# A transformer block on one core: operand roles of the dilation-16 value products, and where the merge factors are applied

## The chip, the cores and the metric

The kernel runs on one core of a Trainium2 chip. Time is device time in microseconds of one launch. A run of this kernel repeats closely: three runs before gave 2552.69, 2554.15 and 2554.9 us, and the median, 2554.15, is the time to be compared. The engines are named as the profile names them: TensorE (PE for the matrix products, PEld for the loads of their weights, the stationary operand), VectorE (DVE), ScalarE (ACT), GpSimd (POOL) and SyncE (SP); the last two start the transfers.

## The reference

One decoder block on 2048 positions of width 1024, all in float32. Its first half normalises the input and projects it once. The columns are shared by two groups of heads: four heads of gated linear attention, and eight softmax heads of width 64 that look at their keys at three dilations. Both results pass one output projection. The second half is a gated feed-forward layer of width 2816 with a causal convolution of width 3.

The change touches the softmax heads alone. For each of the dilations 1, 4 and 16 a query attends to 128 keys back at most, in steps of the dilation. The three results are merged by their softmax denominators:

```python
    s = jnp.where(valid, s + alibi, -jnp.inf)
    m = jnp.max(s, axis=-1, keepdims=True)
    p = jnp.exp(s - m)
    den = jnp.sum(p, axis=-1, keepdims=True)
    o = jnp.einsum('bdhnqk,bdhnke->bdhnqe', p, vw.astype(jnp.float32)) / den
    lse = (m + jnp.log(den))[..., 0]
...
    weights = jax.nn.softmax(jnp.stack(lses, axis=0), axis=0)
    return jnp.einsum('gbsh,gbshe->bshe', weights, jnp.stack(outs, axis=0))
```

So for each query, head and dilation there is one factor, exp(m - M) / (sum over dilations of den * exp(m - M)), by which the unnormalised product of p with the values is multiplied before the three are added. Since it belongs to the query, it may multiply p ahead of the product, or the product behind it.

## The kernel before

**Blocks and streams.** The 2048 positions go in four blocks of 512 (`c` from 0 to 3, `NCH`). For each block there is a projection (`proj`), the mixing (`mix`: two steps of linear attention, `gla`, and then `attn` four times, for the four pairs of softmax heads, `hp`), the output projection (`outproj`) and the feed-forward layer (`ffn`). The wide products of `proj`, `outproj`, `ffn` and `down` all go through `mm3` (lines 318 to 320): each float32 operand is split into a high and a low part, and three products of 128 x 128 by 512 columns take the place of one. They fill most of TensorE's time.

**What sets the order.** `mix` and the wide work are generators. `beside` (line 115) walks through the two in turn: a step of `mix` up to its next `yield`, then a step or more of wide work. This gives the written order. The order that each engine really gets is worked out by a planner that runs over the whole program as it is compiled (line 39): it works with a model of the engines' times, and may put instructions that are free to go ahead of written ones that still wait. Each engine then carries out its own instructions in the order it was given. TensorE's small products of `attn` stand in one queue with the wide ones.

**One pair of heads in `attn`.** Tiles have 128 partitions. `s16[hh]` holds the scores of head `hh` (0 or 1) at dilation 16, with 128 queries on the partitions (32 j + l) and four groups `r4` of `nk` = 32 (c + 1) keys in the free dimension; query position 16 l + 4 j + r4. `s4` and `sn` hold the scores of dilations 4 and 1 for both heads, in 4 x 384 columns: 4 x 192 of each head, or 128 where there are no keys before.

1. Scores are made on TensorE (lines 939 and 888), biased with their maxima taken on VectorE (`TTR`, line 903), and turned to exponentials on ScalarE (`soft`, line 907).
2. The maxima and denominators of dilation 1 and 4 are brought to the query order of dilation 16 (lines 978 to 987, with small products at 981 and 983), and the factors `f` for all three dilations are worked out (lines 988 to 997) on VectorE and ScalarE. Line 997 finishes `f`.
3. In the same step `s16` is transposed on TensorE, four transposes of 128 queries by `nk` keys for each head (`turn` at line 1002, which the profile shows as line 916 with tile `s`), and copied back into `s16` as keys by queries (line 1002, by way of `copy`, lines 195 and 197). This is not dependent on `f`.
4. After a `yield`, the factors of dilations 1 and 4 are brought back to these dilations' own query orders (lines 1005 to 1007, 1017 and 1018). `scale` (line 1009) multiplies `s4` and `sn` by them in place: for each head and each of the four groups one instruction with a scalar per partition (line 1013), 8 for each call, 16 for each pair of heads.
5. `turns` transposes `s4` and `sn` (line 916 with tile `sx`), with a `yield` after each.
6. The value products. Those of dilation 16 (line 1037) have the 32 queries of one (r4, j) as the stationary operand and the 64 values as the moving one. The output is 32 queries (partitions 32 j and up) by 64 values. With two heads, four r4 and four j there are 32 of them; j is the innermost loop. Those of dilations 4 and 1 (`add`, line 1043) have the values as the stationary operand, so that their outputs `O` and `O1` have values on the partitions, the two heads on halves of them.
7. `weigh` (line 1021, its multiplication is line 1025) multiplies the dilation-16 output by its factor, from PSUM into a buffer of the ring `pt`. After a `yield` four transposes (line 1064) bring it to values by queries, ScalarE copies it to the tile `stage` in position order (line 1066), and VectorE adds `O1` and `O` to that (lines 1067 and 1069). The result is stored for `outproj`.

PSUM tiles of `attn` and `gla` come from a pool of four (`psa`), the wide products' from another of four (`psg`).

Of the kernel before, what the change touches and what calls it, by code (L numbers as in the profile page):

```python
# [11 lines left out]
F32 = mybir.dt.float32  # L12
# [3 lines left out]
ALU = mybir.AluOpType  # L16
# [4 lines left out]
P = 128  # L21
T = 512
# [126 lines left out]
class K:  # L149
# [687 lines left out]
    def attn(self, c, hp, ready):  # L837
        nc, D = self.nc, self.D
        nk = 32 * (c + 1)
# [29 lines left out]
        s16 = [self.at.tile([P, T], F32, name="s16", bufs=2) for _ in range(2)]  # L869

        H = [slice(0, 64), slice(64, P)]
# [40 lines left out]
        def turn(n, b0, part, to):  # L912

            ps = self.pa()
            for i in range(b0, 4):
                nc.tensor.transpose(ps[:n, i * P:(i + 1) * P], part(i), self.C("id"))  # L916
            self.copy(to, ps[:n, b0 * P:].rearrange("p (r n) -> p r n", n=P))

        def turns(t, first):

            for k in range(3):
                n = slice(k * P, (k + 1) * P)
                b0 = sum(map(first, range(4))) if k == 1 else 0
                if b0 < 4:
                    turn(P, b0, lambda i: t[:, i, n], t[:, b0:, n])
# [9 lines left out]
        for r4 in range(4):  # L935
            for j in range(4):
                for hh in range(2):
                    r = 4 * j + r4
# [4 lines left out]
        v16 = self.at.tile([P, 16, P], F32, name="v16", tag="kt", bufs=2)  # L943
# [13 lines left out]
        ends = lambda *a: (lambda lo, n: (lo, lo + n))(*span(*a))  # L957
# [32 lines left out]
        f = self.at.tile([P, 2, 3, 4], F32, name="f", bufs=2)  # L990
# [8 lines left out]
        xm = self.at.tile(x4, F32, name="xm", bufs=2)[:, 0:2]  # L999
        nc.vector.tensor_tensor(xm, f[:, :, 2][:, :, None, :].to_broadcast(x2), self.C("s4")[:, None, :, None].to_broadcast(x2), op=ALU.mult)  # L1000
        for hh in range(2):
            turn(nk, 0, lambda i: s16[hh][:, i * nk:(i + 1) * nk], s16[hh][:nk].rearrange("p (r n) -> p r n", n=P))
        yield
        ps = self.pa()
# [2 lines left out]
        nc.vector.tensor_copy(f[:, :, 1], ps[:, 32:40].rearrange("p (a r) -> p a r", r=4))  # L1007

        def scale(t, g, first):
            for hh in range(2):  # L1010
                for i in range(4):
                    lo, hi = ends(i, hh, first, g)
                    nc.vector.tensor_scalar(t[:, i, lo:hi], t[:, i, lo:hi], f[:, hh, g, i:i + 1], None, op0=ALU.mult)

        scale(s4, 1, z4)
        xm = self.at.tile(x4, F32, name="xm", bufs=2)[:, 0:2]
        nc.vector.tensor_tensor(xm, ps[:, 0:32].rearrange("p (a b r) -> p a b r", b=4, r=4), self.C("s1")[:, None, None, :].to_broadcast(x2), op=ALU.mult)
        nc.vector.tensor_reduce(f[:, :, 2], xm, AX.X, ALU.add)
        scale(sn, 2, z1)

        def weigh(out, g):

            t = self.at.tile([P, T], F32, name="pt", tag="pt", bufs=5)
            v = lambda t: t.rearrange("p (r h n) -> p r h n", r=4, h=2)
            nc.vector.tensor_tensor(v(t), v(out), f[:, :, g].rearrange("p h r -> p r h")[:, :, :, None].to_broadcast([P, 4, 2, 64]), op=ALU.mult)
            return t

        cols = lambda r4, hh: slice((2 * r4 + hh) * 64, (2 * r4 + hh + 1) * 64)
        turns(s4, z4)
        yield  # L1030
        turns(sn, z1)
        yield
        O16 = self.pa()
        for hh in range(2):
            for r4 in range(4):
                for j in range(4):
                    nc.tensor.matmul(O16[32 * j:32 * j + 32, cols(r4, hh)], s16[hh][:nk, r4 * P + 32 * j:r4 * P + 32 * j + 32], v16[:nk, 4 * j + r4, H[hh]], start=True, stop=True, skip_group_check=True)  # L1037
        O, O1 = self.pa(), self.pa()
        first = [True] * 4

        def add(o, hh, out, lhsT, rhs):
            k = 2 * (o is o1) + hh
            nc.tensor.matmul(out, lhsT, rhs, start=first[k], stop=False, skip_group_check=True)  # L1043
            first[k] = False
# [8 lines left out]
        for i in range(4):  # L1053
            for z in range(2):
                for o, t, vf, only, g in ((o4, s4, f4, z4, 1), (o1, sn, f1, z1, 2)):
                    for hh in range(2):
                        R = H[place(hh, g)]
                        if not only(i):
                            add(o, hh, o(hh, i)[:, z], vf[R, i, z], t[R, i, P + 64 * z:P + 64 * z + 64])
        acc = weigh(O16, 0)  # L1060
        yield
        O16 = self.pa()
        for r4 in range(4):
            nc.tensor.transpose(O16[:, r4 * P:(r4 + 1) * P], acc[:, r4 * P:(r4 + 1) * P], self.C("id"))
        st = self.at.tile([P, T], F32, name="stage", bufs=2)
        nc.scalar.copy(st.rearrange("p (l j r) -> p r j l", j=4, r=4), O16.rearrange("p (r j l) -> p r j l", r=4, j=4))
        nc.vector.tensor_tensor(st, O1, st, op=ALU.add)
# [301 lines left out]
```

## Time and profile before

| | |
|---|---|
| median of the three runs | 2554.15 us |
| the profiled execution's own time | 2554.95 us |
| its span, first to last instruction | 2553.2 us |
| TensorE products busy | 2529.3 us (99% of the span), 19458 instructions |
| TensorE weight loads busy | 2086.9 us (82%) |
| VectorE busy | 1891.1 us (74%), 4104 instructions |
| ScalarE busy | 1279.0 us (50%) |
| GpSimd busy | 446.5 us (17%) |
| granted TensorE clock | 1.000 |

The profile is of one execution. A row of the groups reads: line, engine, operation, written tile <- read tiles, for TensorE the size of the stationary operand (rows * columns), output partitions x columns, and the count; then the busy time in us and the mean duration of one in ns; then the idle time of the engine ahead of these instructions with what ended it. Products overlap in the array: one record's duration runs from its start to its modelled end, and the next may start long before that, so the busy time of a group is not its count times the mean. A row of the timeline is start and length in us, engine, line, operation, tiles and a count for neighbours put together (with the form of the first). A row of the waits is the engine, tile and line that waited, what it waited for, and then the total in us, the number of times and the longest. A row of a stretch gives its length and, for each engine in the order PE, PEld, DVE, ACT, POOL, busy time and count, then the TensorE clock, the share of the DMA engines and GB/s.

### The profile page before, as it was taken

To read this page: it belongs to the slowest core of one execution; us is meant where nothing else is said; L and a number is where in the kernel's file an instruction comes from. 1 tells how busy PE (TensorE), PEld (TensorE's weight loads), DVE (VectorE), ACT (ScalarE), POOL (GpSimd) and SP (SyncE) were. 2 spreads that over 40 slices of the span, in tenths; PEclk is the share of its full clock that TensorE was granted. 3 is DMA by queue.
4 is the path that set the end of the run, shared out by engine and by line. 5 is a ranking of instruction groups with operands and counts; after the bars stand their busy time and mean duration, and the time that the engine had idled before them with its cause. 6 is when DMAs were issued, how large, how long until landed. Compare 5 with 4: busy or idle time off the path is not lost.

```text
span 2553.2 us, 49701 instructions
## 1 busy us (share of the span) xinstructions
PE 2529.3 (99%) x19458; PEld 2086.9 (82%) x19458; DVE 1891.1 (74%) x4104; ACT 1279.0 (50%) x2633; POOL 446.5 (17%) x814
## 2 busy tenths in 40 slices
PE   7999999999999999999999999999999999999999
PEld 4888888888788888888888888888888888888887
DVE  7678877767788677787977777779777776766665
ACT  5566665666554544454545544445444443433332
POOL 2343332322210000122100000310000003100001
PEclk9999999999999999999999999999999999999999
DMA  8776676665632344455434445643444436432332
GB/s 329 251 259 199 203 250 198 215 202 183 219 120 93 120 142 134 131 190 174 130 120 129 136 145 152 208 150 101 125 147 140 146 104 202 149 98 93 99 99 83
DMA packets 189582, 406.30 MB, mean 159 GB/s; under 512 B 48498, under 2 KB 89380, under 8 KB 188068
## 3 DMA queue, kind: packets, MB, share of 16 engines
q0 software_dynamic: 88096, 308.59, 36.9%
q1 hardware_dynamic: 101252, 94.54, 12.2%
q8 instruction: 153, 2.51, 0.4%
q14 instruction: 81, 0.66, 0.1%
HBM read 341.18 MB, written 61.87 MB: 158 GB/s over the span
## 4 chain that ended last, share of the span: by engine, by line
PE 94%; DVE 2%; DMA 1%; issue 1%; ACT 1%; POOL 0%; SPq 0%; POOLq 0%; DVEq 0%; ACTq 0%
PE psg L318 28%; PE psg L319 27%; PE psg L320 27%; PE psa L916 2%; PE psa L888 2%; PE psa L1043 2%; PE psa L714 2%; PE psa L939 1%; PE psa L1037 1%; PE psa L787 1%; PE psa L786 1%; DMA hlo<-y 0%; PE psa L791 0%; DMA wraw<-in_w_ch_dram 0%; PE psg L1239 0%
## 5 line engine op out<-in xcount | busy, mean ns | idle before, releaser
L318 PE MATMUL psg<-hhi,whi 128*128 128x512 f32 x1968 | 773.6, 394 | 0.5 <-DVE x L1190 0.3
L319 PE MATMUL psg<-hlo,whi 128*128 128x512 f32 x1968 | 769.7, 391 | 0.0
L320 PE MATMUL psg<-hhi,wlo 128*128 128x512 f32 x1968 | 769.2, 391 | 0.0
L252 DVE TENSOR_TENSOR wlo<-wraw,whi 128x1024 fp32r<-128x1024 f32 (+1 forms) x388 | 474.9, 1224 | 209.7 <-ACT whi L251 201.0
L251 ACT CAST whi<-wraw 128x1024 fp32r<-128x1024 f32 (+1 forms) x388 | 407.4, 1050 | 440.5 <-PE psg L319 367.3
L318 PEld LDWEIGHTS psg<-hhi,whi 128*128 128x128 f32 x1968 | 369.5, 188 | 78.9 <-ACT stg L590 0.6
L320 PEld LDWEIGHTS psg<-hhi,wlo 128*128 128x128 f32 x1968 | 369.6, 188 | 77.8 <-issue 0.7
L319 PEld LDWEIGHTS psg<-hlo,whi 128*128 128x128 f32 x1968 | 369.7, 188 | 75.1 <-issue 0.3
L318 PE MATMUL psg<-ghi,whi 128*128 128x512 f32 x744 | 295.7, 398 | 0.2 <-DVE x L1190 0.2
L319 PE MATMUL psg<-glo,whi 128*128 128x512 f32 x744 | 292.1, 393 | 0.6 <-DVE glo L1098 0.6
L320 PE MATMUL psg<-ghi,wlo 128*128 128x512 f32 x744 | 291.9, 392 | 0.0
L246 POOL DMA_DIRECT2D wraw<-in_w_up_dram x176 | 97.2, 552 | 977.5 <-DVE wlo L252 769.9
L1190 DVE SCALAR_TENSOR_TENSOR x<-psg,mod,x 128x512 f32<-128x512 f32 x192 | 143.3, 748 | 118.4 <-PE psg L320 118.1
L319 PE MATMUL psg<-wlo,hhi 128*128 128x512 f32 (+2 forms) x512 | 173.9, 340 | 0.0
L318 PE MATMUL psg<-whi,hhi 128*128 128x512 f32 (+2 forms) x512 | 173.0, 342 | 0.6 <-ACT stg L587 0.6
L320 PE MATMUL psg<-whi,hlo 128*128 128x512 f32 (+2 forms) x512 | 173.4, 341 | 0.0
L318 PEld LDWEIGHTS psg<-ghi,whi 128*128 128x128 f32 x744 | 139.7, 188 | 31.3 <-issue 0.9
L319 PEld LDWEIGHTS psg<-glo,whi 128*128 128x128 f32 x744 | 139.8, 188 | 29.6 <-DVE glo L1098 1.4
L320 PEld LDWEIGHTS psg<-ghi,wlo 128*128 128x128 f32 x744 | 139.7, 188 | 29.5 <-issue 0.2
L1145 ACT ACTIVATE y<-psg,tables_sb 128x512 f32<-128x512 f32 x176 | 136.3, 775 | 5.3 <-PE psg L320 4.8
L1146 DVE SCALAR_TENSOR_TENSOR y<-psg,tables_sb,y 128x511 f32<-128x511 f32 x176 | 131.0, 744 | 3.5 <-ACT y L1145 3.4
L1147 DVE SCALAR_TENSOR_TENSOR y<-psg,tables_sb,y 128x510 f32<-128x510 f32 x176 | 130.9, 744 | 0.6
(276 smaller groups left out, 3595.4 us busy)
## 6 DMA issues: line engine op xcount, KB each, us to landing
wraw<-in_w_up_dram POOLq DMA_DIRECT2D x176, 512.0 KB, 3.8
wraw<-in_w_down_dram POOLq DMA_DIRECT2D x88, 512.0 KB, 3.7
wraw<-in_w_ch_dram POOLq DMA_DIRECT2D x44, 512.0 KB, 4.3
wada<-in_w_ada_dram POOLq DMA_DIRECT2D x64, 256.0 KB, 4.7
wraw<-in_w_tokw_dram POOLq DMA_DIRECT2D x32, 512.0 KB, 5.2
sq<-in_xT_dram POOLq DMA_DIRECT2D x48, 256.0 KB, 5.0
x<-x POOLq DMA_DIRECT2D x48, 256.0 KB, 5.4
v<-v SPq DMA_DIRECT2D x44, 256.0 KB, 4.5
```

Of the source, the lines that this page charges most:

```text
L246: ld = self.dq.dma_start(raw[:, :n], src)
L251: nc.scalar.copy(hi[:, :n], raw[:, :n])
L252: nc.vector.tensor_tensor(lo[:, :n], raw[:, :n], hi[:, :n].bitcast(F32), op=ALU.subtract)
L318: nc.tensor.matmul(ps, wh, hh, start=first and k == 0, stop=False, skip_group_check=shared)
L319: nc.tensor.matmul(ps, wh, hl, start=False, stop=False, skip_group_check=shared)
L320: self.lastmm = nc.tensor.matmul(ps, wl, hh, start=False, stop=k == n - 1, skip_group_check=shared)
L714: nc.tensor.matmul(sp[j:j + w, o + n * w:o + (n + 1) * w], kh[R, k0:k0 + w], qh[R, q0:q0 + w], start=True, stop=True)
L888: nc.tensor.matmul(at(i, hh, o, n)[H[z]], q(H[hh], i, z), key(H[hh], i, k0, n), start=True, stop=True, skip_group_check=True)
L1145: nc.scalar.activation(y, ps, AF.Identity, bias=self.cb[:, b:b + 1], scale=self.cw[:, 2, b:b + 1])
L1146: nc.vector.scalar_tensor_tensor(y[:, 1:], ps[:, :T - 1], self.cw[:, 1, b:b + 1], y[:, 1:], op0=ALU.mult, op1=ALU.add)
L1147: nc.vector.scalar_tensor_tensor(y[:, 2:], ps[:, :T - 2], self.cw[:, 0, b:b + 1], y[:, 2:], op0=ALU.mult, op1=ALU.add)
L1190: nc.vector.scalar_tensor_tensor(x1, ps, self.mod[:, 40 + cb:41 + cb], x1, op0=ALU.mult, op1=ALU.add)
```

## The change

The dilation-16 value products swap their operands. The stationary one is now the values (`nk` keys by 64 values of one head), the moving one the 32 queries of (r4, j); the output has the head's 64 values on partitions 64 hh to 64 hh + 63 and the 32 queries in the columns r4 * 128 + 32 j. It has thereby the layout that the four transposes at line 1064 made, and these are gone, with `weigh`, its buffer and the second PSUM tile `O16`. The `yield` ahead of them stays.

The factor of dilation 16 now multiplies `s16` in place, ahead of its transposes: one multiplication for each head, 128 partitions by 4 x `nk`, with the factor spread over the keys of its group. These two stand behind line 1000 in the step that transposes `s16`.

`scale` has one multiplication for each head in place of four, with the factors of the four groups spread over 192 columns each. In the first block (`c` = 0) the groups without earlier keys are narrower (128 columns): there dilation 4 has one multiplication for each head over 4 x 128, and dilation 1 has two, over 1 x 128 and 3 x 192.

```diff
         nc.vector.tensor_tensor(xm, f[:, :, 2][:, :, None, :].to_broadcast(x2), self.C("s4")[:, None, :, None].to_broadcast(x2), op=ALU.mult)
         for hh in range(2):
+            a = s16[hh][:, 0:4 * nk].rearrange("p (r n) -> p r n", r=4)
+            nc.vector.tensor_tensor(a, a, f[:, hh, 0, :, None].to_broadcast([P, 4, nk]), op=ALU.mult)
+        for hh in range(2):
             turn(nk, 0, lambda i: s16[hh][:, i * nk:(i + 1) * nk], s16[hh][:nk].rearrange("p (r n) -> p r n", n=P))
         yield
...
         def scale(t, g, first):
+            n = sum(map(first, range(4)))
             for hh in range(2):
-                for i in range(4):
-                    lo, hi = ends(i, hh, first, g)
-                    nc.vector.tensor_scalar(t[:, i, lo:hi], t[:, i, lo:hi], f[:, hh, g, i:i + 1], None, op0=ALU.mult)
+                for i0, i1 in ((0, n), (n, 4)):
+                    if i0 < i1:
+                        lo, hi = ends(i0, hh, first, g)
+                        a = t[:, i0:i1, lo:hi]
+                        nc.vector.tensor_tensor(a, a, f[:, hh, g, i0:i1, None].to_broadcast([P, i1 - i0, hi - lo]), op=ALU.mult)
...
-        def weigh(out, g):
-
-            t = self.at.tile([P, T], F32, name="pt", tag="pt", bufs=5)
-            v = lambda t: t.rearrange("p (r h n) -> p r h n", r=4, h=2)
-            nc.vector.tensor_tensor(v(t), v(out), f[:, :, g].rearrange("p h r -> p r h")[:, :, :, None].to_broadcast([P, 4, 2, 64]), op=ALU.mult)
-            return t
-
-        cols = lambda r4, hh: slice((2 * r4 + hh) * 64, (2 * r4 + hh + 1) * 64)
         turns(s4, z4)
...
         for hh in range(2):
             for r4 in range(4):
                 for j in range(4):
-                    nc.tensor.matmul(O16[32 * j:32 * j + 32, cols(r4, hh)], s16[hh][:nk, r4 * P + 32 * j:r4 * P + 32 * j + 32], v16[:nk, 4 * j + r4, H[hh]], start=True, stop=True, skip_group_check=True)
+                    nc.tensor.matmul(O16[H[hh], r4 * P + 32 * j:r4 * P + 32 * j + 32], v16[:nk, 4 * j + r4, H[hh]], s16[hh][:nk, r4 * P + 32 * j:r4 * P + 32 * j + 32], start=True, stop=True, skip_group_check=True)
...
-        acc = weigh(O16, 0)
-        yield
-        O16 = self.pa()
-        for r4 in range(4):
-            nc.tensor.transpose(O16[:, r4 * P:(r4 + 1) * P], acc[:, r4 * P:(r4 + 1) * P], self.C("id"))
+        yield
         st = self.at.tile([P, T], F32, name="stage", bufs=2)
```

## The prediction, made before the change was run

> **What bounds the kernel now.** I read the page first (busy shares and the chain that ended last), then TensorE's waits, then the busy times by stretch.
>
> ```profile
> span 2553.2 us, 49701 instructions
> PE 2529.3 (99%) x19458; PEld 2086.9 (82%) x19458; DVE 1891.1 (74%) x4104; ACT 1279.0 (50%) x2633; POOL 446.5 (17%) x814
> PE 94%; DVE 2%; DMA 1%; issue 1%; ACT 1%; POOL 0%; SPq 0%; POOLq 0%; DVEq 0%; ACTq 0%
> ```
> ```profile
> PE psa L464 <- ACT sq L1232: 14.3, 1, 14.3
> PE psa L531 <- ACT sqr L525: 1.1, 1, 1.1
> PE psg L318 <- DVE x L1190: 0.5, 2, 0.3
> ```
> ```profile
> 1345.00:1605.00 260.00, 260.00 (x2287) 216.09 (x2286) 194.52 (x542) 126.46 (x321) 20.79 (x37) 1.00 0.48 141
> 1850.00:2110.00 260.00, 260.00 (x2248) 216.10 (x2248) 194.61 (x544) 124.12 (x314) 22.45 (x38) 1.00 0.45 133
> ```
>
> The order of TensorE's instructions is the time. It is busy 99% of the span, 94% of the last-ending chain is its own work, and its only long wait (14.3 us) lies before the attention begins. In the two stretches, which hold the heads of blocks 2 and 3, the third number (TensorE busy) equals the length: 260.00 of 260.00. VectorE is busy 194.6 there and TensorE waits for it 0.5 us in the worst of its lines. So an edit counts by what it adds to or takes from TensorE's queue; work on VectorE and ScalarE counts only if TensorE comes to wait for it.
>
> **The products (line 1037), the large term.** Each head pair and block issues 2 x 4 x 4 = 32 products, and there are 16 head pairs and blocks. The four rows below hold 1024 records, so each f32 product is two records (a weight load and a pass, twice), and one run is 64 records. Then come the nearest rows for what is new.
>
> ```profile
> L1037 PE MATMUL psa<-v,s 32*32 32x64 f32 x256 | 4.7, 216 | 0.0
> L1037 PE MATMUL psa<-v,s 96*32 96x64 f32 x256 | 4.4, 220 | 0.0
> L1037 PE MATMUL psa<-v,s 128*32 128x64 f32 x256 | 4.4, 221 | 0.0
> L1037 PE MATMUL psa<-v,s 64*32 64x64 f32 x256 | 4.4, 218 | 0.0
> L714 PE MATMUL psa<-pt 64*64 64x64 f32 x128 | 10.0, 224 | 0.0
> ```
> ```profile
> 2090.92 1.10 PE L1037 MATMUL psa<-v,s 128*32 128x64 f32 x64
> 2091.95 3.06 PE L1043 MATMUL psa<-sx,v 128*64 128x128 f32 x96
> ...
> 2105.75 0.39 PE L320 MATMUL psg<-hhi,wlo 128*128 128x512 f32 x1
> 2105.98 0.60 PE L1064 MATMUL psa<-consts_sb,pt 128*128 128x128 f32 x4
> 2106.34 0.48 PE L318 MATMUL psg<-hhi,whi 128*128 128x512 f32 x1
> 2106.65 0.40 PE L319 MATMUL psg<-hlo,whi 128*128 128x512 f32 x1
> ```
>
> Before, a run of 64 takes 1.10 us although one record lasts 221 ns: (1100 - 221) / 63 = 14 ns from record to record. That pace comes from the output slice. It is 32 partitions at 32j, and j is the innermost loop, so four neighbours use four different column groups of the array and run side by side.
>
> After, the weights are 64 columns of values and the output is partitions 0-63 for all 16 products of the first head, 64-127 for all 16 of the second. j now only moves the output along the free dimension, so neighbours share one column group, and each must wait for the load of the next 64 columns there. The nearest row is line 714's 64*64 form: there four products follow each other in one place of the array (level 64 has one start row, 0). Its 128 records are 8 calls x 2 halves x 8 records, 16 runs: 10.0 / 16 = 0.625 us a run, less the last record's 0.224, over 7 steps: **57 ns** from record to record. It moves 64 columns where the new products move 32, so what sets that pace must be asked: if the moved columns, 32 would be quicker; if the load of 64 weight columns, not. The loads answer:
>
> ```profile
> L1037 PEld LDWEIGHTS psa<-v,s 128*32 128x32 f32 x256 | 3.8, 110 | 0.9 <-DVE glo L1162 0.4 <-issue 0.3 <-DVE y L1146 0.2
> L888 PEld LDWEIGHTS psa<-kw,qn 64*64 64x64 f32 x752 | 26.2, 132 | 7.5 <-issue 4.5 <-PE psg L319 2.8
> L1006 PEld LDWEIGHTS psa<-f,consts_sb 128*128 128x128 f32 x32 | 4.8, 192 | 0.0
> ```
> ```profile
> 2076.71 0.30 PE L1005 MATMUL psa<-xm,consts_sb 128*128 128x32 f32 x2
> 2076.84 0.37 PE L1006 MATMUL psa<-f,consts_sb 128*128 128x8 f32 x2
> 2077.07 0.49 PE L318 MATMUL psg<-hhi,whi 128*128 128x512 f32 x1
> ```
> ```profile
> L1005 PE MATMUL psa<-xm,consts_sb x32: 190/233/273, 414.9 to 2076.7; 128*128 128x32 f32 x32
> ```
>
> From 64 to 128 weight columns a load grows by (192 - 132) / 64 = 0.94 ns a column. Line 1006 moves only 8 columns, yet its two records hold the queue 2077.07 - 2076.84 = 0.23 us, 115 ns each, for 128 weight columns: about 0.9 ns a column again. So 64 columns take 57 to 58 ns, which is line 714's pace; the load sets it and the halved moving side gains nothing. A run after: 63 x 57 + 224 = 3.82 us, 2.72 more than 1.10; times 16: **+43.5 us**. Little separates the four blocks: the rows for 32, 64, 96 and 128 contraction rows lie within 5 ns.
>
> Bounds for this unseen form: if the moved columns set the pace, line 1005 tells it. Two records with 32 columns end 300 ns after the start of the first, the longest lasts 273, so 27 ns apart: 63 x 27 + 224 = 1.93, +0.83 x 16 = +13.2. From above, line 714's whole busy time a record, start and end of each run included, 10.0 / 128 = 78 ns: 5.0, +3.9 x 16 = +62.4. I take 57, the row with the same weight shape in one column group.
>
> [...]
>
> **The transposes of the weighed product (line 1064), removed.** Four hold the queue 2106.34 - 2105.98 = 0.36 us, and the step after the first wide product that follows is 0.31 where the one before was 2105.98 - 2105.75 = 0.23. Together 0.44, times 16: **-7.0 us**.
>
> **The scaling of s16 ahead of its transposes, moved.** The factor reaches the weights before the eight transposes of line 916, so these now wait for line 997 and two multiplications.
>
> ```profile
> 2066.27 0.35 PE L983 MATMUL psa<-md,consts_sb 128*128 128x16 f32 x2
> 2066.47 1.07 PE L916 MATMUL psa<-consts_sb,s 128*128 128x128 f32 x8
> ```
> ```profile
> 2071.27 0.18 DVE L997 TENSOR_TENSOR f<-f,M 128x24 f32<-128x24 f32 x1
> ```
>
> Before, they stand directly behind line 983; the factor is there 5 us later, and the two multiplications add up to 1.4 us. The order on TensorE is a planner's, and it puts work that waits behind wide products: line 1005 needs the same factor and stands at 2076.71, 10.4 us behind line 983, with no idle time; line 531, which waits within its own step, cost 1.1 us in 32. The scaled weights are used at 2090.92, so there is room for the copies too. I count one more break between wide products per head, 0.08 x 16 = **+1.3 us**. Queued behind a late one would be the wide products, hence all of the time; that is a rival below.
>
> **VectorE.**
>
> ```profile
> L252 DVE TENSOR_TENSOR wlo<-wraw,whi 128x1024 fp32r<-128x1024 f32 x380 | 464.5, 1223 | 204.9 <-ACT whi L251 196.2 <-PE psa L461 1.4 <-PE psa L939 1.0
> L1013 DVE TENSOR_SCALAR sx<-sx,f 128x192 f32<-128x192 f32 x216 | 52.4, 316 | 0.0
> L1013 DVE TENSOR_SCALAR sx<-sx,f 128x128 f32<-128x128 f32 x40 | 8.9, 285 | 0.0
> L1025 DVE TENSOR_TENSOR pt<-psa,f 128x512 f32<-128x512 f32 x16 | 11.0, 687 | 3.8 <-PE psa L1037 3.8
> ```
>
> Removed: 52.4 + 8.9 + 11.0 = 72.3 us. Added: two-operand multiplications, by rows 687 ns for 512 and 1223 for 1024, so 1.047 ns an element. Scaling: 48 of 4 x 192 at 0.955, and in block 0 8 of 512 at 0.687, 8 of 128 at 0.285, 8 of 576 at 0.754: 59.6. On s16: 8 each of 128, 256, 384, 512: 8 x (0.285 + 0.419 + 0.553 + 0.687) = 15.6. Net 75.2 - 72.3 = +2.9 us: the fewer, wider instructions save next to nothing, and TensorE's queue covers it. Without that cover it would be +2.9. One ring buffer and one PSUM tile fewer per head, and a shorter way from products to stored output, are costed at nothing: TensorE waits for none of them, and the wide products cover them.
>
> **Sum.** Against the profiled execution's own 2554.95 us (span 2553.2): +43.5 - 7.0 + 1.3 = +37.8, 2592.75. That execution is 0.80 above the runs' median of 2554.15, so **2592.0**.
>
> **Rivals.**
>
> The moved columns set the pace. 27 ns instead of 57: +13.2 - 7.0 + 1.3 = +7.5, **2561.7**. For it: line 1005's second record. Against it: that record's weights could be loaded while the queue was on other work, and line 1006, in a steady stream, shows 115.
>
> The halves of the two heads run side by side (not slower). If neighbours of both column halves overlap and 32 moved columns cost half of 64, the pace is 27 / 2 = 14 ns, as now: the run stays at 1.1 us and only the transposes' 7.0 go: **2547**. It decides below (1.10 + 0.44 - 0.224) / 63 = 21 ns. For it: four groups do overlap in line 1037 today. Against it: all 16 products of one head are written before the other's, and records start in that order. [...]
>
> TensorE waits for the scaled weights. If the planner leaves the transposes behind line 983, each head idles (2071.45 - 2066.47) + 1.4 + 0.2 for line 1000 = 6.6 us: +105, **2697**. A miss by 0.5 to 1.5 us a head would give 2600 to 2616. Against: line 1005.
>
> The change does what it says in any of these; the products can't be left out.
>
> **How the numbers follow.** Forecast (57 ns, no new wait): 0.75. Moved columns: 0.07. Side by side: 0.05. Waits: 0.13, of which 0.03 for the full one. The range 2570 to 2609 leaves out the first two rivals, the full wait and the upper part of the small one, 0.18 in all; above it ends about where the 78 ns bound does (+62.4 - 5.7: 2610.9), below it stops short of the 27 ns one. No change within 0.2%, about what a measurement here can tell, is 2549 to 2559: faster 0.05 (side by side), same 0.03 (moved columns a little cheaper than worked out), slower 0.92.
>
> **What would show it.** Right: line 1037's successor as one block of 64 records of 3.8 us per head, busy near 61 us in all, 55 to 60 ns from record to record, the same in all four blocks; line 1064 gone; TensorE still 99% busy with waits as before; VectorE's busy time within 10 us of 1891. Wrong: a block under 2.5 us (the load is not the limit), idle TensorE time ended by VectorE or a copy at the transposes of s16 (a new wait), or a time more than 10 us away from what the blocks themselves grew by (the planner's order changed elsewhere).

## The result, and the profile after

| | before | after |
|---|---|---|
| median | 2554.53 us (4 runs, 2552.69 to 2555.58) | 2592.7 us (4 runs, 2588.09 to 2597.05) |
| ratio | | 1.015, 95% interval 1.0137 to 1.0162 |
| the profiled execution's own time | 2554.95 us | 2597.05 us |

The change makes the kernel 38 us slower; 2592.0 was forecast. The agreement is better than the reasons behind it: much of what follows is about terms that were left out and happen to cancel.

The page after, the rows that answer to those shown before:

```profile
span 2595.3 us, 49457 instructions
PE 2570.5 (99%) x19394; PEld 2132.5 (82%) x19394; DVE 1891.0 (73%) x3936; ACT 1278.4 (49%) x2633; POOL 441.3 (17%) x814
```

TensorE is still busy 99% of the span, and VectorE's busy time has not moved (1891.1 before). The groups of TensorE by form, the products and what follows them (lines 1035 and 1041 now, 1037 and 1043 before). First the two rows of line 1043 before the change, then the rows after it:

```profile
L1043 PE MATMUL psa<-sx,v 128*64 128x128 f32 x512 | 33.0, 277 | 0.0
L1043 PE MATMUL psa<-sx,v 64*64 64x64 f32 x864 | 22.0, 222 | 0.0
```
```profile
L1041 PE MATMUL psa<-sx,v 128*64 128x128 f32 x512 | 40.8, 318 | 0.0
L1041 PE MATMUL psa<-sx,v 64*64 64x64 f32 x864 | 20.3, 239 | 0.0
L1035 PE MATMUL psa<-s,v 32*64 32x32 f32 x256 | 18.0, 237 | 0.1
L1035 PE MATMUL psa<-s,v 64*64 64x32 f32 x256 | 16.0, 227 | 0.0
L1035 PE MATMUL psa<-s,v 96*64 96x32 f32 x256 | 14.8, 223 | 0.0
L1035 PE MATMUL psa<-s,v 128*64 128x32 f32 x256 | 14.8, 223 | 0.0
```

The 1024 records of the products are there with 32 moved columns, and their busy time has gone from 17.9 to 63.6 us. Blocks 2 and 3 (96 and 128 rows) have 14.8 each; blocks 0 and 1 have more, and in line 1041 one record is longer on the mean than it was in line 1043 (318 against 277 ns, 239 against 222). The timeline of TensorE in the second head pair of block 1 and the last of block 3, and the stretches of the first:

```profile
1005.02 1.03 PE L916 MATMUL psa<-consts_sb,sx 128*128 128x128 f32 x8
1005.98 4.35 PE L1035 MATMUL psa<-s,v 64*64 64x32 f32 x64
1010.26 5.55 PE L1041 MATMUL psa<-sx,v 128*64 128x128 f32 x96
...
2133.00 3.54 PE L1035 MATMUL psa<-s,v 128*64 128x32 f32 x61
2136.32 0.32 PE L1041 MATMUL psa<-sx,v 128*64 128x128 f32 x1
```
```profile
1005.40:1008.80 3.40, 3.40 (x58) 3.23 (x56) 0.69 (x1) 0.59 (x1) 0.53 (x1) 1.00 0.51 157
1008.81:1015.62 6.81, 6.81 (x112) 6.42 (x110) 0.00 (x0) 1.01 (x1) 0.00 (x0) 0.50 0.45 126
1015.64:1019.04 3.40, 3.40 (x24) 2.77 (x19) 2.33 (x3) 0.01 (x1) 0.00 (x0) 1.00 0.22 63
```

In block 3 the first 61 records take 3.54 us: (3540 - 223) / 60 = 55 ns apart, against 57 forecast. In the head pair of block 1 all 64 take 4.35 us, where the undisturbed ones take 3.71. The number after POOL's, the granted TensorE clock, tells why: it is 1.00, then 0.50 for 6.81 us, then 1.00 again. Before the change it was 1.00 throughout. TensorE's record was busy all of the 3.40 us ahead of the drop, but all that it did there was the end of the transposes and most of the new products.

The profiled execution has five such stretches, at 421.7 (13.65 us), 503.6 (3.41), 643.6 (3.41), 1008.8 (6.83) and 1080.5 (6.83): 34.1 us at half clock, all in blocks 0 and 1. That is why the mean clock of the span is 0.993, and why the runs spread: their times and mean clocks are 2588.09 (0.997), 2591.27 (0.995), 2594.14 (0.994) and 2597.05 (0.993).

TensorE's waits, and the transposes of s16 in the last head pair, which now stand ahead of lines 1008 and 1009 (1005 and 1006 before):

```profile
PE psa L464 <- ACT sq L1226: 14.4, 1, 14.4
PE psa L916 <- DVE sx L1019: 2.5, 4, 1.7
```
```profile
2116.84 0.39 PE L320 MATMUL psg<-hhi,wlo 128*128 128x512 f32 x1
2117.08 1.03 PE L916 MATMUL psa<-consts_sb,s 128*128 128x128 f32 x8
2117.95 0.31 PE L1008 MATMUL psa<-xm,consts_sb 128*128 128x32 f32 x2
2118.09 0.37 PE L1009 MATMUL psa<-f,consts_sb 128*128 128x8 f32 x2
2118.31 0.49 PE L318 MATMUL psg<-hhi,whi 128*128 128x512 f32 x1
```

No transpose of s16 waits for the multiplications; the planner has put them 10 us later, as was expected: line 983 begins at 2106.76 here, the transposes at 2117.08. But it has joined them to another group of small products in place of making a new break between wide ones. The one new wait is at the transposes of s4 and sn in the very first head pair, 2.0 of the 2.5 us, where VectorE is still busy with other work and with the scaling.

### The profile page after: what moved, and what is told of

It is laid out like the page before. It is cut to its first block, busy times and chain, and to the rows that moved or that the text cites. A ratio compares the mean times of both kernels' runs of the same rounds, so it can differ in the third digit from the quotient of the medians.

```text
span 2595.3 us, 49457 instructions
## 1 busy us (share of the span) xinstructions
PE 2570.5 (99%) x19394; PEld 2132.5 (82%) x19394; DVE 1891.0 (73%) x3936; ACT 1278.4 (49%) x2633; POOL 441.3 (17%) x814
## 4 chain that ended last, share of the span: by engine, by line
PE 54%; issue 0%; POOL 0%; DVE 0%; POOLq 0%
PE psg L318 16%; PE psg L319 16%; PE psg L320 16%; PE psa L1035 1%; PE psa L916 1%; PE psa L888 1%; PE psa L1041 1%; PE psa L714 1%; PE psa L939 0%; PE psa L787 0%; PE psa L786 0%; PE psa L791 0%; PE psa L817 0%; PE psa L464 0%; PE psa L696 0%
```

## The experiments

The theory: the load of 64 weight columns in one column group sets the pace of the new products; the rest of the time is the half clock that follows them. The rivals: the moved columns, or a fixed price of a record, set the pace; or the time comes from the other parts of the change (waits for scaled weights, the order of the queue). Each ratio is to runs of the kernel before on the same chip (medians 2554.23, 2553.76 and 2553.44 us in the three groups).

### The products put back

```diff
-  matmul(O16[H[hh], r4 * P + 32 * j:...+ 32], v16[:nk, 4 * j + r4, H[hh]], s16[hh][:nk, ...])
+  matmul(O16[32 * j:32 * j + 32, cols(r4, hh)], s16[hh][:nk, ...], v16[:nk, 4 * j + r4, H[hh]])
...
+  acc = self.at.tile([P, T], F32, name="pt", tag="pt", bufs=5)
+  nc.vector.tensor_copy(acc, O16)
   yield
+  O16 = self.pa()
+  for r4 in range(4):
+      nc.tensor.transpose(O16[:, r4 * P:(r4 + 1) * P], acc[:, r4 * P:(r4 + 1) * P], self.C("id"))
```

> The products of dilation 16 take back the weights of the softmax as stationary operand (and with them a copy out of PSUM and the four transposes); the factors stay ahead of the transposes of s16 and the scaling stays one instruction per head. If the products alone cost the time (load of 64 weight columns in one column group, and the half clock that follows them in blocks 0 and 1): blocks of 64 records take 1.0 to 1.1 us again, the granted clock is 1.000, and the time is 2554 to 2558 us. If the waits for the scaled weights or the changed order of the queue cost a part: the clock is back and the blocks are short, but 2562 us or more.

Measured: 2558.89 us, ratio 1.0019 (1.0009 to 1.0028). This lies between the two expected ranges, 0.9 us above the first one: the blocks are short again (1.1 us but for the first head pair), but the clock is not back in every run (0.998 to 1.000 in the ten). So 34 of the 38 us belong to the products and what they bring with them, and 4.7 us stay against the kernel before. The profile shows where a part of them lies: the wait at the transposes of sx is there as in the changed kernel, and behind it a stretch at half clock. The two runs whose clock was 1.000 took 2556.58 and 2556.82 us.

```profile
PE psa L916 <- DVE sx L1019: 2.5, 4, 1.7
```
```profile
423.56:430.37 6.81, 6.81 (x103) 5.66 (x104) 6.73 (x13) 4.75 (x8) 3.92 (x7) 0.50 0.65 212
```

### One scaling per head, alone

The kernel before, with the new `scale` only.

> The kernel before with one part of the change alone: one multiplication per head in place of four where dilations 4 and 1 are scaled. VectorE's busy time is expected within 3 us of 1891 and TensorE to wait for none of it: 2551 to 2558 us. If the wider instructions help or hold up TensorE: a difference of over 5 us, with idle time of TensorE that VectorE ends.

Measured: 2554.53 us, ratio 1.0001 (0.9992 to 1.001). No difference that this can tell. Its wide multiplications cost 951 ns each (948 in the changed kernel), where 955 had been worked out.

### The factors ahead, alone

The kernel before, with s16 multiplied ahead of its transposes and a copy in place of `weigh`.

> The kernel before with one part of the change alone: the factor of dilation 16 multiplies s16 ahead of its transposes, and a plain copy takes the place of the weighing behind the products. If this part made the wait of TensorE for VectorE in the first head pair of products_back: the wait at the transposes of sx (about 2 us) and a stretch at half clock are there again, 2556 to 2561 us. If it needs the single scaling per head as well: no such wait, 2552 to 2556 us.

Measured: 2555.9 us, ratio 1.0007 (0.9998 to 1.0016), which doesn't tell it from no change. The wait is there, so it comes with this part:

```profile
PE psa L916 <- DVE sx L1016: 2.7, 2, 2.1
```

The half clock behind it did not follow in this profile, whose run had a clock of 1.000; six of the ten runs had 0.998 or 0.999. So the time fell into the range of "no such wait" although the wait is there.

### The two heads in turn

```diff
-        for hh in range(2):
-            for r4 in range(4):
-                for j in range(4):
+        for r4 in range(4):
+            for j in range(4):
+                for hh in range(2):
```

> The changed kernel with the two heads as the innermost loop of the products, so that neighbours use the two column halves in turn. If each half has its own load of 64 columns (57 ns) and the halves run side by side: 29 ns from record to record, a block of 2.05 us in place of 3.6, -24 us, and fewer stretches at half clock: 2556 to 2569 us. If records go one after another whatever the column group: 3.6 us blocks and 2588 to 2597 us. If the moved columns set the pace: 14 ns, 1.1 us blocks, about 2548 us.

Measured: 2563.69 us, ratio 1.0032 (1.002 to 1.0043). A block in the timeline of TensorE:

```profile
2103.14 2.06 PE L1035 MATMUL psa<-s,v 128*64 128x32 f32 x64
```

(2060 - 223) / 63 = 29 ns, where the changed kernel has 55 in one column group, with the same instructions. The two column halves of the array do run side by side here, where neighbours use both: 29 ns against 55. This also rules out that a record costs the same whatever column group its neighbour uses. A fixed price of a record within one column group is left for the next run.

### 128 weight columns, and twice the moved columns

The first takes `v16[:nk, 4 * j + r4, :]` as the stationary operand of each product and writes all 128 partitions; the second moves the 64 columns of j and its neighbour. What each leaves out of the dilation-16 result is said in its expectation.

> The changed kernel with 128 value columns (both heads' values) as the stationary operand of each product, so that the output is 128 partitions and the second head's products write over the first's: the merge of the two heads at dilation 16 is thereby left out. If the load of the weight columns sets the pace: 0.9 ns times 128, 112 to 115 ns from record to record, blocks of 7.2 us, about 58 us more than the changed kernel, 2640 to 2655 us. If the pace of 57 ns is a fixed price of a record in one column group: blocks of 3.6 us and 2585 to 2597 us.

> The changed kernel with each product moving 64 columns in place of 32 (those of its neighbour j as well, written over by it, so half of the queries get the product of the wrong keys: the dilation-16 part is computed wrongly there). If the load of 64 weight columns sets the pace: 57 to 59 ns from record to record as with 32 columns, blocks of 3.6 us, and as the array moves columns all the time, less half clock: 2576 to 2592 us. If the moved columns set it: over 100 ns, blocks of 6.5 us or more, over 2630 us.

Measured: 2721.6 us with 128 weight columns, 2589.14 with twice the moved ones (one run each). The groups and stretches with 128 weight columns, then the groups with twice the moved columns:

```profile
L1035 PE MATMUL psa<-s,v 128*128 128x32 f32 x256 | 41.0, 332 | 0.0
```
```profile
1481.60:1488.40 6.80, 6.80 (x60) 6.58 (x58) 2.03 (x3) 1.53 (x2) 0.53 (x1) 1.00 0.25 81
1488.43:1495.24 6.81, 6.81 (x47) 6.75 (x48) 0.00 (x0) 1.02 (x1) 0.00 (x0) 0.50 0.19 52
```
```profile
L1035 PE MATMUL psa<-s,v 96*64 96x64 f32 x256 | 15.1, 224 | 0.0
L1035 PE MATMUL psa<-s,v 128*64 128x64 f32 x256 | 15.1, 224 | 0.0
```

Moving 64 columns in place of 32 changes 14.8 to 15.1 us: the moved columns are not the limit. Doubling the weight columns doubles the time of a record: from record start to record start the median is 112 ns in the head pairs that ran mostly at full clock, against 58 in the changed kernel, as 115 had been read from line 1006 before. That rules out a fixed price of a record in one column group too. At half clock it is 213, 1.9 times as much. The time missed its range from above because blocks 2 and 3 now run into half clock as well (0.94 on the mean in 1390 to 1650, 0.96 in 1920 to 2180, where the changed kernel has 1.00): the mean clock of the span was 0.967, so by an estimate 0.033 x 2719.8 = 90 us of the 2721.6 are its price. The 2632 that are left would lie 8 us below the range.

### Rows filled with zeros

In blocks 0 and 1 the products contract over 128 rows, the added ones zero.

> The changed kernel, but in blocks 0 and 1 (32 and 64 keys) the products run over all 128 rows, with zeros in the added rows of the values and of the weights (set by GpSimd and VectorE). If the half clock comes from the few rows in use: granted clock 1.000 in blocks 0 and 1 as in blocks 2 and 3, same pace of 57 to 58 ns, 2574 to 2584 us. If it comes from the length of the stretch with small products, or from TensorE's wait in the first head: stretches at half clock remain, clock 0.993 to 0.997, 2587 to 2598 us.

Measured: 2596.3 us, ratio 1.0164 (1.0149 to 1.0179), clock 0.996 to 0.997. It does not answer the question cleanly. The zeroing on VectorE delays the scaling, so TensorE waits 10.2 us at the transposes of sx in block 0, and block 0 keeps two stretches at half clock. Block 1 has none. The time fell into the second range. But a stretch appears in block 2, in a head pair that the edit leaves as it was:

```profile
1424.09 3.55 PE L1041 MATMUL psa<-s,v 96*64 96x32 f32 x61
```
```profile
1424.08:1427.48 3.40, 3.40 (x64) 3.39 (x64) 1.69 (x2) 0.32 (x1) 0.53 (x1) 1.00 0.14 39
1427.50:1430.89 3.39, 3.39 (x37) 3.39 (x36) 0.00 (x0) 1.01 (x1) 0.00 (x0) 0.50 0.64 217
```

Here the products began at 1424.09, and 3.4 us later the clock fell from 1.00 to 0.50. In the changed kernel this head pair did not lose its clock (1.00 in 1390 to 1650). So a drop came with 96 rows in use too. Where the product block lies may matter as well. In the profile of the changed kernel all stretches begin and end a whole number of 3.413 us apart: they begin 81.92, 221.87, 587.09 and 658.77 us after the first, 24, 65, 172 and 193 times 81.92 / 24 = 3.413. The products of this head pair run there from 1427.21 to 1430.92, across a mark of that grid (1428.64); in the run here they fill the 3.40 us ahead of the drop. That their place decides is not shown by a run of its own.

### A step of wide work between the heads

> The changed kernel with a step of wide work written between the products of the first head and those of the second (one more yield in each head pair), all products as in the changed kernel. If the half clock follows a window of 3.41 us that holds little else than these products: no window is filled by 1.8 us of them, half clock stays at most in the very first head pair, clock 0.998 or more, and the time is 2578 to 2587 us. If it comes from the small products as such, wherever they stand: 0.993 to 0.997 and 2587 to 2597 us.

Measured: 2617.0 us, ratio 1.0247 (1.0233 to 1.0261). Expected by neither: the planner closed the gap again in blocks 0 and 1 (runs of 3.6 us and longer), and the extra steps shifted the whole interleaving of mixing and wide work, with 10 us more of idle TensorE time and a mean clock of 0.991. The edit did not make the case that it was to test.

### Moved columns between the heads

```diff
         for hh in range(2):
+            for _ in range(2 if hh and c < 2 else 0):
+                matmul(O16[H[1], :], self.C("id")[:, H[1]], self.cond[:, 0:T], ...)
```

> The changed kernel with two extra products of 512 moved columns (1.7 us of TensorE) between the first head's products and the second's in blocks 0 and 1, written into columns that the second head's products then write over; the result is the same. If the clock is halved after a window of 3.41 us in which few columns move: the four stretches at half clock in head pairs 1, 3, 5 and 6 of the changed kernel go, only the one in the first head pair (behind TensorE's wait) stays, clock 0.997 to 0.998; time 8 x 1.7 = 14 us more for the products and some 8 us less for the clock, 2594 to 2602 us. If the clock goes by the count or the form of the small products: clock 0.993 to 0.996 still, 2603 to 2610 us.

Measured: 2602.43 us (2 runs), ratio 1.0191 (1.0173 to 1.021). The two runs differ: the profiled one took 2598.01 us with a clock of 1.000 and no stretch at half clock, the other 2606.85 with 0.996. So the filling does not keep the clock up in every run (more on this in the last section). But the profiled run serves another purpose: it is the changed kernel at full clock, with known additions. The order of its queue is that of the changed kernel but for 40 of 19394 records, and the wait at the transposes of sx is the same 2.5 us.

### Four column groups

Each product is cut in two along its values, with the four groups as the innermost loop:

```diff
+        for r4 in range(4):
+            for j in range(4):
+                for n0 in range(0, P, 32):
+                    N, q0 = slice(n0, n0 + 32), r4 * P + 32 * j
+                    matmul(O16[N, q0:q0 + 32], v16[:nk, 4 * j + r4, N], s16[n0 // 64][:nk, q0:q0 + 32], ...)
```

> The changed kernel with each product cut in two along its values: 32 value columns as stationary operand, 64 products in place of 32 per head pair and block, and the four column groups of the array as the innermost loop. If the load of the weight columns sets the pace in each column group and the groups run side by side: 32 columns at 0.9 ns are 28 ns, in four groups 7 ns from record to record, 128 records in 1.1 to 1.3 us, so the block is as short as before the change and the four transposes are gone: 7 us less than products_back, 2550 to 2554 us. If a record costs the same whatever its weights (28 ns with two groups in turn, as heads_alternate showed): 128 records in 3.8 us, 2590 us or more.

Measured: 2552.46 us, ratio 0.9996 (0.9987 to 1.0005). The groups and a block of the timeline:

```profile
L1036 PE MATMUL psa<-s,v 64*32 64x32 f32 x512 | 5.2, 195 | 0.0
L1036 PE MATMUL psa<-s,v 96*32 96x32 f32 x512 | 5.2, 198 | 0.0
L1036 PE MATMUL psa<-s,v 128*32 128x32 f32 x512 | 5.2, 198 | 0.0
```
```profile
1462.19 1.30 PE L1036 MATMUL psa<-s,v 96*32 96x32 f32 x128
```

(1300 - 198) / 127 = 8.7 ns: twice the records of the changed kernel in a third of the time, with values still stationary. With four groups in turn that is 4 x 8.7 = 35 ns from record to record in one group, where 0.9 ns for each of 32 columns would be 28. It is some 40 us faster than the changed kernel. From the kernel before it can't be told apart. In its profile the transposes' 6.3 us are gone, but the products hold the queue 3.7 us longer than before, TensorE waits 2.5 us at line 916 and 3.5 us in the products of dilations 4 and 1 (line 1042), and 6.83 us in the first head pair run at half clock. Two more aimed at the first head pair.

> quarters with the scaling of dilations 4 and 1 as before the change (four instructions per head): if the single scaling is what makes TensorE wait in the first head pair (2.5 us at the transposes of sx, then 6.8 us at half clock), both go and the time is 2547 to 2550 us; if the factor ahead of s16 is enough for it, the wait is about 2 us again and the time within 2 us of quarters, 2551 to 2554 us.

> quarters with the multiplication of s16 on GpSimd in place of VectorE. If the place of these multiplications in VectorE's queue makes the wait in the first head pair: the wait and the half clock behind it go, 2547 to 2550 us. If GpSimd, which also starts the weights' transfers, is late with them: TensorE waits at the transposes of s16 instead, 2554 us or more.

Measured: with four instructions 2551.07 us, ratio 0.999 (0.9982 to 0.9999), with the wait still there (2.7 us), as the second case had it; and with s16 multiplied on GpSimd 2549.9 us, ratio **0.9985** (0.9976 to 0.9994), with a shorter wait, 1.1 of these 2.0 us in the first head pair:

```profile
PE psa L916 <- DVE sx L1019: 2.0, 4, 0.8
```

Here the clock in the runs was 0.999 or 1.000; the profile has 3.41 us at half clock, early in the kernel, and none in the attention. Against the kernel before, this version is 3.5 us of 2553.44 faster, about half of the 6.3 us that the transposes held. Its interval leaves out 1, but it overlaps those of the two other versions with four column groups, so that GpSimd brought this is not shown. The time fell into the expected range, but the wait, which was to go, only became shorter.

## Why the prediction was right

**The account.** Adding up the times from one TensorE record's start to the next, line by line, gives what each group holds of the queue. At full clock ("filled", profiled, without its extra products) against before:

| | forecast | full clock | profiled run after |
|---|---|---|---|
| products (16.7 us before) | +43.5 | +43.0 | +44.6 |
| `add`, the products of dilations 4 and 1 (51.8) | 0 | -4.7 | +5.8 |
| transposes behind the products | -7.0 | -6.3 | -6.3 |
| wide products of 512 columns | +1.3 | -6.1 | -5.8 |
| transposes of s16, s4 and sn | 0 | +4.2 | +4.2 |
| all the rest, idle time too | 0 | -2.0 | -0.4 |
| sum | +37.8 | +28.1 | +42.1 |

The last line is the difference of the spans: 2596.2 - 14.9 - 2553.2 for "filled", 2595.3 - 2553.2 after. Between the columns lie 14 us, the price of the half clock in the profiled run; at the median it is about 2592.7 - (2598.01 - 14.9) = 9.6.

**The products** were right in size and reason. 57 ns from record to record was forecast from line 714's form of the same weight shape; 55 to 58 was measured. That the load of the weight columns sets it, and not the moved ones, is shown by three runs: 128 weight columns 112 ns, 64 moved columns the same pace, two column groups in turn 29 ns.

**The step that failed**: "the rows for 32, 64, 96 and 128 contraction rows lie within 5 ns", so that "little separates the four blocks". It took a full clock for granted in all four. Blocks 0 and 1 lost it in five of their eight head pairs, and most of the price fell on the work behind the products: by the account above `add` holds 5.8 + 4.7 = 10.5 us more of the queue than at full clock, the products 44.6 - 43.0 = 1.6. Before the change the granted clock was 1.00 in every stretch of the attention, so no row could have priced it; but the forecast named no such rival either.

**The new break** ("one more break between wide products per head", +1.3) had the wrong sign. The planner did move the transposes of s16 behind wide work without idle time, as forecast, but joined them to lines 1008 and 1009. Between them and the lost transposes behind the products, the queue changes from wide to small work some 270 times where it did so 322 times (counted over all records), and the wide products gained 6.1 us. That the one makes the other is not shown: the single scaling alone left 28 changes fewer and gained nothing on the wide products.

**What follows the products** was costed at nothing, and at full clock gained 4.7 us. The trace shows where: before, the planner had put the `add` products of seven head pairs of blocks 1 to 3 in an order that mixes those with 128 rows and those with 64, and they held the queue 3.39 to 3.85 us there, against 2.99 in the five others. The last head pair of block 2 is one of the seven (the last of block 3, with the 3.06 us that the prediction shows, is not):

```profile
1584.83 3.92 PE L1043 MATMUL psa<-sx,v 128*64 128x128 f32 x96
```

At full clock after the change all twelve hold it 2.99 to 3.02 us. The swap itself is not needed for a part of this: with the single scaling alone `add` gains 2.3 us. Such gains of order can't be read from the rows of one kernel.

**The transposes** at -7.0 were -6.3 in their own time; the rest would be in the time of the wide products. **VectorE** at +2.9 was -0.1 in busy time. Neither of its parts alone moved the time by more than its interval, but both together did (4.7 us in "The products put back"); the wait in the first head pair and the half clock behind it, which were costed at nothing, are a part of that. TensorE's largest row of waits for VectorE before was 0.6 us (line 319) and not 0.5, which changes nothing. The wait rival was seen on a small scale, 2.5 us, at the transposes of sx and not at those of s16. The side-by-side rival was rightly unlikely for the loop as written, and its mechanism is real: two groups in turn gave 29 ns, four groups 8.7 and a kernel that is not slower.

So the forecast missed about -10 us at full clock (`add` and the wide products, less 4.2 us for the transposes of s16, s4 and sn, which are spread over the head pairs) and +10 to +14 us of half clock. The range covered it; that the middle was hit is luck, because the two cancel.

## What to carry to other kernels

Count a small product by its weight load when its moving side is narrow: here about 0.9 ns a weight column with 64 and 128 of them (58 and 112 ns). What hid it here is a neighbour in another column group (29 ns with two groups in turn, 8.7 with four), so swapping operands must be judged together with the innermost loop. Before moving work into one corner of the array, look at the granted clock in the stretches: here four of sixteen head pairs, with 3.7 us of such work each, ran into 3.4 to 6.8 us at half clock, and a fifth, behind a wait, into 13.7. And before taking a right total as a right account, add up the queue line by line.

## What the runs showed of the hardware

In 1005.40 to 1008.80 of the profile after, TensorE's records filled 3.40 of 3.40 us and its weight loads 3.23, and the granted clock then fell from 1.00 to 0.50 for 6.81 us: being busy all the time did not keep it up there. In the first head pair the interval ahead of the drop was one of waiting instead (1.42 us busy of 3.40):

```profile
418.30:421.70 3.40, 1.42 (x11) 1.21 (x11) 3.40 (x7) 1.17 (x3) 0.00 (x0) 1.00 0.56 225
421.72:435.35 13.63, 13.63 (x188) 12.38 (x186) 7.82 (x15) 6.71 (x11) 7.16 (x12) 0.50 0.74 246
```

The five stretches of the profile after were 3.41, 6.83 and 13.65 us long, 1, 2 and 4 times 3.413, and its record of the clock has no values but 0.5 and 1. The run with 128 weight columns and 32 moved ones, whose record was as full (6.80 of 6.80 us ahead of a drop), was at half clock far more: a mean clock of 0.967, against 0.993 with 64.

One sum sets the intervals ahead of a drop apart from the others. Cut the fourteen profiles, from 100 us on, into intervals of 3.413 us on the grid of their own stretches (of the drop behind the last instruction where there is no stretch inside), and add up for each interval at full clock the columns that TensorE's records move, each record's columns times its rows / 128. The median interval holds 7680. Of 34 intervals with under 1600, 33 were followed by half clock; of 72 with 1600 to 3100, seven; of 9947 with more, none. In the profile after, the five drops follow 496, 1344, 1408, 1488 and 1920, while one interval of 1744 and two others of 1920 were followed by full clock. So in these profiles a drop goes with how little is moved through the rows, be it by waiting (1408 ahead of the drop in the first head pair) or by weight loads (1344 in 1005.40 to 1008.80). This fits the runs above: the drops of the changed kernel came with 32 and 64 rows in use, one came with 96 (1616 in "Rows filled"), and moved columns between the heads kept the clock up in one run of two. No run changed this sum alone, and why the intervals between 1600 and 3100 go either way stays open.
